# Down products in groups of four tiles, done between the Strassen pairs of the next group, and accumulators dealt out anew

## The chip, the core and the metric

The kernel runs on one core of a Trainium2 chip. The metric is the device time of one execution in microseconds; before the change the median of 3 runs is 2069.6 us (2067.61 to 2075.72).

## What is computed

A decoder trunk of two layers with model width 1024, on 512 tokens, float32. Each layer adds half a feed-forward, a mixer, and half a feed-forward again:

```python
x = x + 0.5 * swiglu_ffn(rmsnorm(x, g1), w_gu1, w_down1)
x = x + mixer(rmsnorm(x, gm))
x = x + 0.5 * swiglu_ffn(rmsnorm(x, g2), w_gu2, w_down2)
def swiglu_ffn(x, w_gu, w_down):
    gate, up = jnp.split(x @ w_gu, 2, axis=-1)
    return (jax.nn.silu(gate) * up) @ w_down
```

The hidden width is 2816, which is 22 tiles of 128. The change touches the feed-forward alone; it runs four times (stages f0a, f0b, f1a, f1b). The two mixers, the norms and the inputs are as they were.

## The kernel before, in words

The residual lies in X, eight tiles of 128 channels by 512 tokens. Every float32 product is made of three matmuls (`mm3`, L177 to L179): operands are split into a high part, written by ACT, and a low part, the DVE difference; weight-high times x-high, weight-high times x-low, weight-low times x-high.

A feed-forward (`ffn`) makes 22 hidden tiles. The first four (CLASSIC) are plain: gate and up are 24 matmuls of 512 columns each, and `hidden` makes the tile. The other 18 are *pairs* (class `Pair`): gate and up of one hidden tile are made together by seven Strassen-Winograd products (B11, Q7, Q6, B21, Q4, Q5, B22), each 12 matmuls of 256 columns, so 84 a pair. They multiply combinations of the four weight quarters, made on DVE in `load` (L311 to L313) from raw blocks that four DMAs bring (L307 to L310), with combinations of the activation quarters, made once per feed-forward by `Quarters.before` and `Quarters.after` (split at L260 to L264, combined at L269 to L282). `load` then makes four split weights ("jobs", L320 on ACT and L321 on DVE) in tiles given by `parts`, a ring of five. There are raw blocks for two pairs.

A pair has three accumulators: a and b from the ring `psum()` of PSB = 5, e from `psum2()` of 3. p1 makes a, and ACT copies it to b (L338). p7 makes e, copied to the upper half of t2 (L349). p6 goes on a, copied to the lower half of t2 (L354). p2 goes on b, and ACT takes its silu (L343). p4 goes on e, and DVE adds half of e to t2 (L359). p5 goes on a, ACT copies it to the free half of b (L364), and DVE adds that to t2 (L365). p3 goes on a; ACT takes the silu (L370), DVE multiplies (L372), and `down` writes the hidden tile's high part on ACT (L390) and its low part on DVE (L391).

Hidden tiles live in a ring of eight (NH). So the 22 tiles are done in groups of 8, 8 and 6: all pairs of a group, then the whole down product of the group: for each of the eight X tiles one accumulator over the group's tiles (24 or 18 matmuls of 512 columns), its weights by `wload` (L163, L171, L172), and one DVE addition into X (L458). Stages in the order of time are then: 4 pairs (after the 4 plain tiles), down of 8, 8 pairs, down of 8, 6 pairs, down of 6. The third product p3 of a pair comes after p1 and p7 of the next one (`left`); the last pair of a group ends p5, p4, p3.

The order on PE is the program's order (`manual_schedule(engines=PE_ONLY)`). On ACT, DVE and the queues a planner orders the instructions ahead of time by a modelled time and a priority; `high_priority(offset=n)` gives an instruction the priority of one n places earlier. Offsets: raw blocks and combinations RAHEAD = 400, splits SAHEAD = 230 (180 and 110 for the first two pairs), evictions EV = 320, the hidden tile's multiply and split 160, `wload` 90. Each engine then runs its list in that order, whatever the chip's real times.

Of the kernel before, what the change touches and what calls it, by code (L numbers as in the profile page):

```python
# [12 lines left out]
P = 128  # L13
T = 512
# [42 lines left out]
def build(tc, a, out, stages=("f0a", "ab", "f0b", "f1a", "nsa", "f1b")):  # L57
    nc = tc.nc
    with ExitStack() as ctx:
# [16 lines left out]
        def blk(i, dt, name):  # L76
            return bp.tile([P, BW.get(i, 4 * T)], dt, name=name, tag=f"b{i}")
# [8 lines left out]
        def psum():  # L86
            return pp.tile([P, T], F32, name="ps", bufs=PSB)
# [33 lines left out]
        def roots(after):  # L121

            nc.scalar.activation(warm, after[:, 0:1], AF.Sqrt, scale=0.0, bias=eps)
# [42 lines left out]
        def wload(src, n=CW, eng=None):  # L166
            with tc.high_priority(offset=AHEAD):
                raw = wraw(src, n)
                hi = wp.tile([P, CW], F32R, name="whi")
                lo = wp.tile([P, CW], F32R, name="wlo")  # L170
                nc.scalar.activation(hi[:, :n], raw[:, :n], AF.Copy)  # L171
                (eng or nc.vector).tensor_sub(lo[:, :n], raw[:, :n], hi[:, :n].bitcast(F32))  # L172
            return hi, lo

        def mm3(ps, wh, wl, xh, xl, start, stop, on=False):

            nc.tensor.matmul(ps, wh, xh, start=start, stop=False, skip_group_check=on)  # L177
            nc.tensor.matmul(ps, wh, xl, start=False, stop=False, skip_group_check=on)  # L178
            nc.tensor.matmul(ps, wl, xh, start=False, stop=stop, skip_group_check=on)  # L179
# [116 lines left out]
        class Pair:  # L296
# [1 line left out]
            def __init__(self, Q, down):  # L298
                self.Q, self.down, self.W = Q, down, {}

            def load(self, w, rb, first=False):
                with tc.high_priority(offset=RFIRST if first else RAHEAD):
                    ra, rc = (blk(rb[2 * (turns[1] % 2) + i], F32, f"r{i}")[:, :4 * T]
                              .rearrange("p (s c) -> p s c", s=4) for i in range(2))
                    turns[1] += 1

                    nc.sync.dma_start(ra[:, 0], w[0][:, :T])  # L307
                    nc.sync.dma_start(rc[:, 3], w[1][:, :T])
                    nc.sync.dma_start(ra[:, 3], w[1][:, T:])
                    nc.sync.dma_start(rc[:, 0], w[0][:, T:])  # L310
                    nc.vector.tensor_add(ra[:, 1:3], ra[:, 0:4:3], rc[:, 3:4].to_broadcast([P, 2, T]))  # L311
                    nc.vector.tensor_add(rc[:, 1], ra[:, 0], ra[:, 2])
                    nc.vector.tensor_add(rc[:, 2], rc[:, 0], rc[:, 1])  # L313
                with tc.high_priority(offset=SFIRST if first else SAHEAD):
                    for src, names in ((ra[:, 0:2], ("B11", "Q7")), (rc[:, 0:2], ("B21", "Q6")),
                                       (ra[:, 2:4], ("Q5", "Q4")), (rc[:, 2:3], ("B22",))):
                        hi, lo = parts()
                        m = len(names) * T
                        src = src.rearrange("p s c -> p (s c)")
                        nc.scalar.activation(hi[:, :m], src, AF.Copy)  # L320
                        nc.vector.tensor_sub(lo[:, :m], src, hi[:, :m].bitcast(F32))  # L321
                        for n, name in enumerate(names):
                            self.W[name] = hi[:, n * T:(n + 1) * T], lo[:, n * T:(n + 1) * T]
                return self
# [7 lines left out]

            def p1(self):

                self.a, self.b, self.t1 = psum(), psum(), tp.tile([P, T], F32, name="t1", bufs=3)
                self.product(self.a, "B11", True)
                with tc.high_priority(offset=EV):
                    nc.scalar.activation(self.b[:, :H], self.a[:, :H], AF.Copy)  # L338
# [16 lines left out]

            def p4(self):
                self.product(self.e, "Q4", False)
                with tc.high_priority(offset=EV):
                    nc.vector.tensor_add(self.t2[:, :H], self.e[:, :H], self.t2[:, :H])  # L359

            def p5(self):
                self.product(self.a, "Q5", False)
                with tc.high_priority(offset=EV):
                    nc.scalar.activation(self.b[:, H:], self.a[:, :H], AF.Copy)  # L364
                    nc.vector.tensor_add(self.t2[:, H:], self.b[:, H:], self.t2[:, H:])  # L365

            def p3(self):
                self.product(self.a, "B22", False)
# [6 lines left out]
        def ffn(gname, wgu, wd, x, lay, nxt, first=None):  # L375
# [30 lines left out]
            for j in range(CLASSIC):  # L406
# [19 lines left out]
                    quarters.before()  # L426
                if j >= 2:
                    hidden(*wait.pop(0))
            quarters.after()

            left = []
            j0 = 0
            while j0 < JT:
                j1 = min(JT, j0 + NH)
                js = list(range(max(CLASSIC, j0), j1))
                with tc.manual_schedule(engines=PE_ONLY):
                    if js[0] == CLASSIC:

                        p, q = (Pair(quarters.Q, downs(j)).load(wgu[j], rb, True) for j in js[:2])
                        for f in (p.p1, p.p7, p.p6, q.p1, q.p7, p.p2, p.p4, p.p5, q.p6, p.p3, q.p2, q.p4, q.p5):  # L440
                            f()
                        left = [q.p3]
                        js = js[2:]
                    for j in js:
                        p = Pair(quarters.Q, downs(j)).load(wgu[j], rb)
                        end = j == j1 - 1
                        for f in (p.p1, p.p7, *left, p.p6, p.p2, *((p.p5, p.p4, p.p3) if end else (p.p4, p.p5))):
                            f()
                        left = [] if end else [p.p3]
                if j1 == JT:  # L450
                    roots(hpart(JT - 1)[0].bitcast(F32))
                for i in range(KT):
                    ps = psum()
                    hi, lo = wload(wd[i, :, j0 * P:j1 * P], (j1 - j0) * P)
                    for k in range(j1 - j0):
                        mm3(ps, hi[:, k * P:(k + 1) * P], lo[:, k * P:(k + 1) * P], *hpart(k),
                            k == 0, k == j1 - j0 - 1)
                    nc.vector.scalar_tensor_tensor(X[i], ps, 0.5, X[i], op0=OP.mult, op1=OP.add)  # L458
                    if j1 == JT:
                        nxt(i)  # L460
                j0 = j1

        def out_proj(w, yh, yl, nxt, lead):

# [818 lines left out]
```

## Time and profile before

| | |
|---|---|
| median of 3 runs | 2069.6 us |
| the profiled execution | 2072.72 us, span 2071.0 us |
| PE / PEld busy | 1991.6 / 1735.3 us |
| DVE / ACT / POOL busy | 1373.8 / 1028.7 / 278.0 us |
| mean granted TensorE clock | 0.985 of full |
| four feed-forwards, from the first pair on | 59.6 to 381.1, 656.4 to 965.6, 1011.4 to 1318.9, 1746.8 to 2053.7 us |

Busy times are shares of one execution; a line such as L177 is that of a helper and is told apart by the operand (h: down product; qB, qQ: pairs; x: plain tiles and projections). Times of a timeline row are the start and the length; in square brackets stands the idle time of the engine before it, and what ended that.

### The profile page before, as it was taken

How to read it: one execution, taken by the hardware profiler on the slowest of the kernel's cores; microseconds unless marked ns; L12 is line 12 of the kernel's file. 1: busy time of each engine (PE TensorE's matmuls, PEld its weight loads, DVE VectorE, ACT ScalarE, POOL GpSimd, SP SyncE). 2: the span in 40 equal slices, each digit the busy share in tenths (PEclk: the TensorE clock that was granted, in tenths of full speed). 3: DMA queues.
4: the chain of work that ended last, by engine and by line, in shares of the span. 5: the costliest groups of instructions: out<-in, count | busy, mean ns of one | idle time of the engine just before them, and what ended most of it. 6: DMA issues, size and time to landing. Idle time of an engine off the chain costs nothing.

```text
span 2071.0 us, 30532 instructions
## 1 busy us (share of the span) xinstructions
PE 1991.6 (96%) x11896; PEld 1735.3 (84%) x11896; DVE 1373.8 (66%) x2189; ACT 1028.7 (50%) x1900; POOL 278.0 (13%) x290
## 2 busy tenths in 40 slices
PE   8899899989999998999999999999999999999997
PEld 6889898867788998897989889877777768999896
DVE  6847657489758658475956746433877778657474
ACT  5525436355545445254535435334878755445252
POOL 3000000343020000002000000202655530000002
PEclk9999999999999999999999999999999999999998
DMA  5232322322222333233232323321101032323222
GB/s 184 83 101 82 112 79 77 99 72 87 82 97 89 115 90 112 69 110 109 84 112 85 111 85 113 106 90 51 34 16 32 16 107 81 113 87 108 87 62 87
DMA packets 74736, 182.09 MB, mean 88 GB/s; under 512 B 8416, under 2 KB 9184, under 8 KB 74592
## 3 DMA queue, kind: packets, MB, share of 16 engines
q1 hardware_dynamic: 74448, 180.06, 28.0%
q8 instruction: 93, 1.52, 0.3%
q14 instruction: 51, 0.42, 0.1%
q10 hardware_dynamic: 144, 0.09, 0.0%
HBM read 178.02 MB, written 2.10 MB: 87 GB/s over the span
## 4 chain that ended last, share of the span: by engine, by line
PE 60%; DVE 9%; DMA 4%; issue 3%; ACT 2%; POOL 0%; SPq 0%; POOLq 0%; DVEq 0%; ACTq 0%
PE ps L177 14%; PE ps L178 14%; PE ps L179 14%; DMA r<-wgu 3%; PE pt L179 3%; PE pt L177 3%; PE pt L178 3%; PE px L994 2%; PE pt L789 2%; PE pt L1010 1%; DVE wx L321 1%; PE ps L954 1%; PE pt L1011 1%; DVE wlo L172 1%; DVE wlo L321 1%
## 5 line engine op out<-in xcount | busy, mean ns | idle before, releaser
L171 ACT ACTIVATE whi<-raw 128x1024 fp32r<-128x1024 f32 (+2 forms) x196 | 193.2, 987 | 363.9 <-PE ps L178 251.6
L178 PE MATMUL ps<-h,whi 128*128 128x512 f32 x704 | 277.5, 394 | 1.2 <-DVE h L391 1.2
L177 PE MATMUL ps<-h,whi 128*128 128x512 f32 x704 | 275.8, 392 | 1.0 <-ACT h L390 1.0
L179 PE MATMUL ps<-h,wlo 128*128 128x512 f32 x704 | 275.9, 392 | 0.0
L320 ACT ACTIVATE whi<-r 128x1024 fp32r<-128x1024 f32 (+1 forms) x174 | 165.6, 952 | 194.3 <-PE ps L178 156.5
L172 DVE TENSOR_TENSOR wlo<-raw,whi 128x1024 fp32r<-128x1024 f32 (+2 forms) x166 | 192.4, 1162 | 73.3 <-ACT whi L171 68.4
L118 POOL TENSOR_TENSOR acc<-acc,t 128x512 f32<-128x512 f32 x48 | 74.6, 1555 | 1136.4 <-ACT t L116 1131.2
L458 DVE SCALAR_TENSOR_TENSOR X<-ps,X 128x512 f32<-128x512 f32 x96 | 66.4, 691 | 231.0 <-PE ps L179 231.0
L321 DVE TENSOR_TENSOR wlo<-r,whi 128x1024 fp32r<-128x1024 f32 (+1 forms) x174 | 188.8, 1087 | 23.0 <-ACT whi L320 22.5
L177 PE MATMUL ps<-x,whi 128*128 128x512 f32 x432 | 179.0, 414 | 0.9 <-ACT x L106 0.9
L311 DVE TENSOR_TENSOR r<-r,r 128x1024 f32<-128x1024 f32 x72 | 88.9, 1236 | 134.2 <-DMA r<-wgu 134.0
L179 PE MATMUL ps<-x,wlo 128*128 128x512 f32 x432 | 171.1, 396 | 0.0
L178 PE MATMUL ps<-x,whi 128*128 128x512 f32 x432 | 170.7, 395 | 0.4 <-DVE x L107 0.3
L177 PEld LDWEIGHTS ps<-h,whi 128*128 128x128 f32 x704 | 132.9, 189 | 31.4 <-ACT h L390 1.9
L178 PEld LDWEIGHTS ps<-h,whi 128*128 128x128 f32 x704 | 132.9, 189 | 30.5 <-DVE h L391 2.4
L179 PEld LDWEIGHTS ps<-h,wlo 128*128 128x128 f32 x704 | 132.7, 188 | 28.5
L177 PE MATMUL ps<-qB,whi 128*128 128x256 f32 x520 | 145.8, 280 | 3.4 <-ACT ps L364 3.4
L179 PE MATMUL ps<-qB,wlo 128*128 128x256 f32 x520 | 145.1, 279 | 0.3 <-DVE wlo L321 0.3
L178 PE MATMUL ps<-qB,whi 128*128 128x256 f32 x520 | 145.2, 279 | 0.0
L321 DVE TENSOR_TENSOR wx<-r,wx 128x1024 fp32r<-128x1024 f32 (+1 forms) x114 | 123.4, 1083 | 22.4 <-ACT wx L320 19.2
L390 ACT ACTIVATE h<-t 128x512 fp32r<-128x512 f32 x88 | 55.4, 630 | 144.7 <-DVE t L372 142.1
L320 ACT ACTIVATE wx<-r 128x1024 fp32r<-128x1024 f32 (+1 forms) x114 | 107.2, 941 | 6.1 <-DVE r L311 4.1
(340 smaller groups left out, 5457.3 us busy)
## 6 DMA issues: line engine op xcount, KB each, us to landing
r<-wgu SPq DMA_DIRECT2D x288, 256.0 KB, 3.7
raw<-wd SPq DMA_DIRECT2D x64, 512.0 KB, 3.6
raw<-wgu SPq DMA_DIRECT2D x30, 512.0 KB, 3.5
raw<-wd SPq DMA_DIRECT2D x32, 384.0 KB, 3.1
raw<-ab_fm SPq DMA_DIRECT2D x21, 512.0 KB, 3.5
raw<-nsa_fm SPq DMA_DIRECT2D x17, 512.0 KB, 3.4
raw<-ab_out SPq DMA_DIRECT2D x8, 512.0 KB, 3.5
raw<-nsa_out SPq DMA_DIRECT2D x16, 256.0 KB, 2.7
```

The source lines that it names most:

```text
L118: nc.gpsimd.tensor_add(acc, acc, sq)
L171: nc.scalar.activation(hi[:, :n], raw[:, :n], AF.Copy)
L172: (eng or nc.vector).tensor_sub(lo[:, :n], raw[:, :n], hi[:, :n].bitcast(F32))
L177: nc.tensor.matmul(ps, wh, xh, start=start, stop=False, skip_group_check=on)
L178: nc.tensor.matmul(ps, wh, xl, start=False, stop=False, skip_group_check=on)
L179: nc.tensor.matmul(ps, wl, xh, start=False, stop=stop, skip_group_check=on)
L311: nc.vector.tensor_add(ra[:, 1:3], ra[:, 0:4:3], rc[:, 3:4].to_broadcast([P, 2, T]))
L320: nc.scalar.activation(hi[:, :m], src, AF.Copy)
L321: nc.vector.tensor_sub(lo[:, :m], src, hi[:, :m].bitcast(F32))
L390: nc.scalar.activation(hh, t2, AF.Copy)
L458: nc.vector.scalar_tensor_tensor(X[i], ps, 0.5, X[i], op0=OP.mult, op1=OP.add)
L789: nc.tensor.matmul(p2[m][:, :155].rearrange("p (g n) -> p g n", g=5), w[:, q * 256 + m * P:q * 256 + (m + 1) * P], tt[:, :, n:n + 8 * 30 + ...
```

## The change

`load` can be made in two parts, so that a down weight's tile can be taken between the first job and the other three. Accumulator b comes from the ring of three. The copy after p5 goes to the free half of e, and `second` makes one 512-wide addition of e to t2 when both p4 and p5 are done. `quarters.after` has a priority 120 places earlier. The function `two` loads the down weights of two X tiles for a group of four hidden tiles in one transfer, splits them, and gives two functions, each an accumulator of 12 matmuls and one addition into X. They are called between the products of the pairs: tiles 0 to 3 in the first four pairs, tiles 4 to 7 in pairs 8 to 11, and so on to tiles 12 to 15 in pairs 16 to 19; pairs 20 and 21 have none. The down product of tiles 16 to 21 follows at the end as before.

```diff
-            def load(self, w, rb, first=False):
...
+            def load(self, w, rb, first=False, part=0):
...
+                    self.jobs = [(ra[:, 0:2], ("B11", "Q7")), (rc[:, 0:2], ("B21", "Q6")),
+                                 (ra[:, 2:4], ("Q5", "Q4")), (rc[:, 2:3], ("B22",))]
...
+                    for src, names in (self.jobs, self.jobs[:1], self.jobs[1:])[part]:
...
-                self.a, self.b, self.t1 = psum(), psum(), tp.tile([P, T], F32, name="t1", bufs=3)
+                self.a, self.b, self.t1 = psum(), psum2(), tp.tile([P, T], F32, name="t1", bufs=3)
...
             def p4(self):
                 self.product(self.e, "Q4", False)
-                with tc.high_priority(offset=EV):
-                    nc.vector.tensor_add(self.t2[:, :H], self.e[:, :H], self.t2[:, :H])
+                self.second()
...
-                    nc.scalar.activation(self.b[:, H:], self.a[:, :H], AF.Copy)
-                    nc.vector.tensor_add(self.t2[:, H:], self.b[:, H:], self.t2[:, H:])
+                    nc.scalar.activation(self.e[:, H:], self.a[:, :H], AF.Copy)
+                self.second()
+
+            def second(self):
+
+                self.n = getattr(self, "n", 0) + 1
+                if self.n == 2:
+                    with tc.high_priority(offset=EV):
+                        nc.vector.tensor_add(self.t2, self.e, self.t2)
...
+            with tc.high_priority(offset=120):
+                quarters.after()
+
+            def two(i, j0, j1):
+
+                n = (j1 - j0) * P
+                with tc.high_priority(offset=SAHEAD):
+                    raw = wp.tile([P, CW], F32, name="raw", bufs=2)[:, :2 * n]
+                    nc.sync.dma_start(raw.rearrange("p (i c) -> p i c", i=2),
+                                      wd[i:i + 2, :, j0 * P:j1 * P].rearrange("i p c -> p i c"))
+                    hi, lo = parts()
+                    nc.scalar.activation(hi[:, :2 * n], raw, AF.Copy)
+                    nc.vector.tensor_sub(lo[:, :2 * n], raw, hi[:, :2 * n].bitcast(F32))
+
+                def one(m):
                     ps = psum()
...
+                        ks = slice(m * n + k * P, m * n + (k + 1) * P)
+                        mm3(ps, hi[:, ks], lo[:, ks], *hpart(j0 + k), k == 0, k == j1 - j0 - 1)
+                    nc.vector.scalar_tensor_tensor(X[i + m], ps, 0.5, X[i + m], op0=OP.mult, op1=OP.add)
+
+                return lambda: one(0), lambda: one(1)
+
+
+            G = 4
+            with tc.manual_schedule(engines=PE_ONLY):
+
+                p = Pair(quarters.Q, downs(CLASSIC)).load(wgu[CLASSIC], rb, True)
+                q = Pair(quarters.Q, downs(CLASSIC + 1))
+                q.load(wgu[CLASSIC + 1], rb, True, 1)
+                d = two(0, 0, G)
+                q.load(None, None, True, 2)
+                e = two(2, 0, G)
+                for f in (p.p1, p.p7, p.p6, q.p1, d[0], d[1], p.p2, q.p7, p.p4, p.p5, q.p6, p.p3, e[0], q.p2, e[1],
+                          q.p4, q.p5):
+                    f()
+                left = [q.p3]
+                for j in range(CLASSIC + 2, JT):
+                    p = Pair(quarters.Q, downs(j)).load(wgu[j], rb)
+                    j0 = min(j // G * G, JT - JT % G - G)
+                    i = 2 * (j - j0)
+                    d = two(i, j0 - G, j0) if i < KT else ((lambda: None),) * 2
+                    rest = (p.p5, p.p4, p.p3) if j == JT - 1 else (p.p4, p.p5)
+                    for f in (p.p1, p.p7, *left, d[0], p.p6, p.p2, d[1], *rest):
+                        f()
+                    left = [p.p3]
+            roots(hpart(JT - 1)[0].bitcast(F32))
```

Taken out is the loop over groups quoted in words above (pairs of a group, then its down product); the down product at the end keeps its form, with `hpart(j0 + k)`.

## Rows read from the trace of the kernel before

**Rows 1.** The page, part 1 (engines) and part 4 (chain that ended last).
```profile
PE 1991.6 (96%) x11896; PEld 1735.3 (84%) x11896; DVE 1373.8 (66%) x2189; ACT 1028.7 (50%) x1900; POOL 278.0 (13%) x290
...
PE 60%; DVE 9%; DMA 4%; issue 3%; ACT 2%; POOL 0%; SPq 0%; POOLq 0%; DVEq 0%; ACTq 0%
```

**Rows 2.** Waits of PE: who, for whom, us in total, times, longest.
```profile
PE ps L179 <- DVE wx L321: 10.8, 7, 2.1
...
PE ps L177 <- ACT ps L364: 10.0, 8, 2.7
...
PE ps L177 <- ACT t L354: 5.7, 3, 3.9
```

**Rows 3.** Windows of the four-pair stages: engine busy us (count), PEclk, DMA; sum.
```profile
59.60:108.70 49.10, 43.18 (x338) 42.44 (x338) 41.28 (x52) 27.42 (x47) 0.00 (x0) 0.93 0.35 100
...
656.40:695.90 39.50, 39.50 (x337) 39.29 (x336) 34.54 (x44) 27.42 (x46) 0.00 (x0) 1.00 0.30 94
...
sum 169.30, PE 162.14 PEld 160.58 DVE 147.75 ACT 107.65 POOL 0.00; mean PE 40.54 PEld 40.14 DVE 36.94 ACT 26.91 POOL 0.00
```

**Rows 4.** Windows of the four eight-pair stages, their sum and mean.
```profile
sum 343.60, PE 323.71 PEld 320.26 DVE 257.12 ACT 191.81 POOL 0.00; mean PE 80.93 PEld 80.06 DVE 64.28 ACT 47.95 POOL 0.00
```

**Rows 5.** Windows of the four six-pair stages, their sum and mean.
```profile
sum 243.10, PE 237.57 PEld 236.00 DVE 177.41 ACT 139.14 POOL 1.38; mean PE 59.39 PEld 59.00 DVE 44.35 ACT 34.78 POOL 0.34
```

**Rows 6.** Windows of the eight down stages of eight tiles; first, and sum.
```profile
108.70:152.60 43.90, 43.90 (x194) 36.03 (x193) 17.90 (x21) 9.41 (x11) 0.00 (x0) 1.00 0.35 105
...
sum 355.20, PE 354.09 PEld 289.89 DVE 144.76 ACT 73.79 POOL 0.00; mean PE 44.26 PEld 36.24 DVE 18.10 ACT 9.22 POOL 0.00
```

**Rows 7.** Windows of the four down stages of six tiles, their sum.
```profile
sum 133.90, PE 132.83 PEld 108.03 DVE 79.60 ACT 66.54 POOL 34.62; mean PE 33.21 PEld 27.01 DVE 19.90 ACT 16.64 POOL 8.65
```

**Rows 8.** Timeline of DVE in an eight-pair stage: start, us, instruction, idle.
```profile
232.84 1.23 DVE L311 TENSOR_TENSOR r<-r,r 128x1024 f32<-128x1024 f32 x1 [3.95 <-DMA r<-wgu]
...
233.98 0.69 DVE L372 TENSOR_TENSOR t<-t,t 128x512 f32<-128x512 f32 x1
...
236.32 0.68 DVE L391 TENSOR_TENSOR h<-t,h 128x512 fp32r<-128x512 f32 x1
```

**Rows 9.** Timeline of ACT, the same place.
```profile
229.03 0.39 ACT L370 ACTIVATE t<-ps 128x256 f32<-128x256 f32 x1
```

**Rows 10.** The page, part 5: two DVE groups, busy and mean ns, idle before.
```profile
L458 DVE SCALAR_TENSOR_TENSOR X<-ps,X 128x512 f32<-128x512 f32 x96 | 66.4, 691 | 231.0 <-PE ps L179 231.0
...
L311 DVE TENSOR_TENSOR r<-r,r 128x1024 f32<-128x1024 f32 x72 | 88.9, 1236 | 134.2 <-DMA r<-wgu 134.0
```

**Rows 11.** Waits of SP's own queue, the longest in total.
```profile
SPq L163 <- DVE wlo L172: 689.4, 153, 23.9
```

**Rows 12.** Groups by form: the 128x256 pieces of a pair's end.
```profile
L365 DVE TENSOR_TENSOR t<-ps,t 128x256 f32<-128x256 f32 x72 | 30.0, 417 | 4.3 <-ACT ps L364 4.3
...
L364 ACT ACTIVATE ps<-ps 128x256 f32<-128x256 f32 x72 | 26.5, 368 | 17.9 <-PE ps L179 17.9
```

**Rows 13.** Timeline of PE, first four-pair stage: wait for Q4.
```profile
72.35 0.38 PE L177 MATMUL pt<-qQ,whi 128*128 128x256 f32 x1 [3.90 <-ACT qQ L263]
```

**Rows 14.** Timeline of DVE there: low part of tile 3, Q4 subtract.
```profile
67.76 0.69 DVE L391 TENSOR_TENSOR h<-t,h 128x512 fp32r<-128x512 f32 x1
...
68.97 1.22 DVE L279 TENSOR_TENSOR xn<-xn,xn 128x1024 f32<-128x1024 f32 x1
```

**Rows 15.** Timeline of DVE, fourth feed-forward: the same tile's low part.
```profile
1754.16 0.69 DVE L391 TENSOR_TENSOR h<-t,h 128x512 fp32r<-128x512 f32 x1
```

**Rows 16.** Timeline of ACT at two group ends: silu of the last product.
```profile
109.71 0.36 ACT L370 ACTIVATE t<-ps 128x256 f32<-128x256 f32 x1
...
2020.95 0.39 ACT L370 ACTIVATE t<-ps 128x256 f32<-128x256 f32 x1 [0.69 <-PE ps L179]
```

**Rows 17.** Timeline of DVE at the same two: the hidden tile, low part.
```profile
112.71 0.69 DVE L391 TENSOR_TENSOR h<-t,h 128x512 fp32r<-128x512 f32 x1 [0.70 <-ACT h L390]
...
2023.29 0.68 DVE L391 TENSOR_TENSOR h<-t,h 128x512 fp32r<-128x512 f32 x1
```

More of the change, by code (lines that the diff above doesn't have):

```diff
@@ L299, in __init__ @@
                 self.Q, self.down, self.W = Q, down, {}
-            def load(self, w, rb, first=False):
[L302 to L313, printed above, removed]
+            def load(self, w, rb, first=False, part=0):
+                if part < 2:
+                    with tc.high_priority(offset=RFIRST if first else RAHEAD):
+                        ra, rc = (blk(rb[2 * (turns[1] % 2) + i], F32, f"r{i}")[:, :4 * T]
+                                  .rearrange("p (s c) -> p s c", s=4) for i in range(2))
+                        turns[1] += 1
+                        nc.sync.dma_start(ra[:, 0], w[0][:, :T])
+                        nc.sync.dma_start(rc[:, 3], w[1][:, :T])
+                        nc.sync.dma_start(ra[:, 3], w[1][:, T:])
+                        nc.sync.dma_start(rc[:, 0], w[0][:, T:])
+                        nc.vector.tensor_add(ra[:, 1:3], ra[:, 0:4:3], rc[:, 3:4].to_broadcast([P, 2, T]))
+                        nc.vector.tensor_add(rc[:, 1], ra[:, 0], ra[:, 2])
+                        nc.vector.tensor_add(rc[:, 2], rc[:, 0], rc[:, 1])
+                    self.jobs = [(ra[:, 0:2], ("B11", "Q7")), (rc[:, 0:2], ("B21", "Q6")),
+                                 (ra[:, 2:4], ("Q5", "Q4")), (rc[:, 2:3], ("B22",))]
                 with tc.high_priority(offset=SFIRST if first else SAHEAD):
-                    for src, names in ((ra[:, 0:2], ("B11", "Q7")), (rc[:, 0:2], ("B21", "Q6")),
-                                       (ra[:, 2:4], ("Q5", "Q4")), (rc[:, 2:3], ("B22",))):
+                    for src, names in (self.jobs, self.jobs[:1], self.jobs[1:])[part]:
                         hi, lo = parts()
@@ L428, in ffn @@
                     hidden(*wait.pop(0))
[L429 to L452, printed above, removed]
+            with tc.high_priority(offset=120):
+                quarters.after()
@@ L453, in ffn @@
                     ps = psum()
-                    hi, lo = wload(wd[i, :, j0 * P:j1 * P], (j1 - j0) * P)
                     for k in range(j1 - j0):
[L456 to L461, printed above, removed]
+                        ks = slice(m * n + k * P, m * n + (k + 1) * P)
@@ L463, in out_proj @@
+            roots(hpart(JT - 1)[0].bitcast(F32))
+            for i in range(KT):
+                ps = psum()
+                hi, lo = wload(wd[i, :, j0 * P:], (JT - j0) * P)
+                for k in range(JT - j0):
+                    mm3(ps, hi[:, k * P:(k + 1) * P], lo[:, k * P:(k + 1) * P], *hpart(j0 + k),
+                        k == 0, k == JT - j0 - 1)
+                nc.vector.scalar_tensor_tensor(X[i], ps, 0.5, X[i], op0=OP.mult, op1=OP.add)
+                nxt(i)
         def out_proj(w, yh, yl, nxt, lead):
```

## The prediction

> **What bounds the kernel now.** I read the page's engine line and chain first: PE is busy for 96% of the span, and 60% of the chain that ended last is PE, while DVE, DMA and "issue" have 9%, 4% and 3% [rows 1]. PE's work is not changed by this edit, so all that can be gained is time in which PE waits or runs at the lower clock inside the feed-forwards. The waits of PE name DVE's low parts of weights (10.8 us) and ACT copies and evictions (10.0 and 5.7 us) as the largest [rows 2]; all of these belong to pairs.
>
> Next I cut the four feed-forwards into stages and compared each kind of stage with its best member. The best four-pair stage takes 39.50 us, and there PE is busy throughout [rows 3]; that is 9.875 us a pair and 1.41 us a product. An eight-tile down stage takes 43.90 us for 192 matmuls [rows 6], which is 0.2286 us each, 2.74 us for twelve of them, and 32.9 us for the 144 of a six-tile stage. Against these floors: the four-pair stages 169.3 - 158.0 = 11.3 us [rows 3]; the eight-pair stages 343.6 - 316.0 = 27.6 us [rows 4]; the six-pair stages 243.1 - 237.0 = 6.1 us [rows 5]; the eight-tile down stages 355.2 - 351.2 = 4.0 us [rows 6]; the six-tile ones 133.9 - 131.7 = 2.2 us [rows 7]. Together 51.2 us, the most that better order in the feed-forwards can give. More than half lies in the eight-pair stages. Of the first stage's share, 9.6 us are f0a's alone (49.1 against 39.5): a wait of 3.90 us for the quarter Q4 [rows 13], and a mean granted clock of 0.93 where the best stage has 1.00 [rows 3], so that some 7 us ran at 1.2 instead of 2.4 GHz.
>
> Why a long run of pairs loses time can be seen on DVE. It isn't short of capacity: 257.1 us in 32 pairs, 8.0 us a pair, against 9.875 [rows 4]. But its list is in order, and at L311 it stands idle for the raw blocks, 134 us over 72 pairs [rows 10]. In one instance it waits 3.95 us, and the multiply of the pair before, whose silu was begun at 229.03, comes only behind that at 233.98 [rows 8, 9]. A block is reloaded only when its splits are done, these need a weight tile that PE gives back, and the two-pair buffer leaves no room when a pair lasts 9.9 us. So the pair stages run at the latency of that loop, not at the rate of an engine.
>
> **What the change does, part by part.**
>
> *Pairs stretched.* A pair with two down pieces takes 9.875 + 2 x 2.74 = 15.4 us. DVE's share becomes 8.0 + 1.24 (one more 128x1024 subtraction, priced as L311 [rows 10]) + 2 x 0.69 (two additions into X [rows 10]) - 0.16 (a 512-wide addition, near 0.69, for two of 0.417 [rows 12]) = 10.5 us, 68%. ACT has 191.8 / 32 = 6.0 us a pair [rows 4] and gets one more split, so under 8 of 15.4. Each pair and its down weight take five jobs, the length of the ring, so each job meets the tile freed a pair earlier, a lead of 7 to 14 us. A DMA wait of 4 us at L311 is then covered. I count the eight-pair loss as gone, 27.6 us, and two thirds of the six-pair loss, 4.1 us (pairs 20 and 21 have no down piece, and 2.0 us stay). The eight-tile down stages vanish as stages, and with them 4.0 us of start-up waits and low clock. The six-tile stage stays, with its 2.2.
>
> *More additions into X.* Forty instead of 24 per feed-forward: 64 x 0.69 = 44 us more on DVE in all [rows 10]. The cover is the 32% of DVE left in the slot, and five accumulators: two pairs hold a, two down pieces the others, one is spare. If that cover fails PE waits up to 0.69 us a piece. I take nothing.
>
> *Transfers.* The down weights are as many transfers as before, 16 of 512 KB and eight of 384 KB per feed-forward, but they are now issued between the raw blocks of the pairs on SP's one queue. SP already spends 689 us waiting for the raw tile to come free, up to 23.9 us at once [rows 11], and what is queued behind such a wait is the next pair's four blocks. They are wanted a pair and a half later, so I take nothing; the other end is in the third rival.
>
> *First two pairs.* The four pieces of 2.74 us stand ahead of p2 and of the last products, and `quarters.after` moves up. In f0a the Q4 subtract stood behind other work until 68.97 [rows 14]; PE now wants Q4 only after 59.6 + 7 x 1.41 + 5.5 = 75 us, which is late enough. New is that the first piece needs hidden tile 3: its low part is wanted four products and ten matmuls after the stage's start, 5.6 + 2.3 = 7.9 us. Before, it was finished after 8.85 us in f0a (67.76 + 0.69 - 59.6) and 8.05 us at the latest in the other three (1754.16 + 0.69 - 1746.8) [rows 14, 15], and the quarters now come in front of it. I keep 4.5 of f0a's 9.6 us (between 1.0, the tile as late as it was, and 9.6) and add 0.4 us to each other first stage, 1.2 us. Gone: 5.1.
>
> *Accumulator b in the ring of three.* Where two pairs are open at the start, p.b, p.e and q.b hold the ring, and q.p7 must wait for p.b, so for the silu right behind p2: 0.37 us of ACT [rows 12] and two hand-overs, about 0.6 us, four times, 2.4 us. The bounds are 0.37 and the longest wait of PE for such an ACT step, 2.7 us [rows 2]. In later pairs at most e of the last pair, b and e are alive: no wait.
>
> *The copy after p5 goes into e.* Normally nobody follows closely. In a feed-forward's last pair p4 is behind p5, and p4 writes the half of e beside the one that ACT is filling. If it has to wait: 0.5 us, four times, 2.0 us, from 0.37 for the copy [rows 12]; if not, nothing; at worst the ACT wait of 2.7 and p4's own 1.41 more, 16 us for four. I take 2.0. The Trainium skill, PSUM — Partial Sum Buffer, section "PSUM bank collisions raise a hardware error", says to guard by bank and quadrant, not by address: by that p4 waits and the 2.0 us stand, by address the sum is 2 us lower. No row here shows which.
>
> *Down right behind the group's last p3.* This is the large new cost. Pairs 8, 12 and 16 run p3 of the last pair of the group and then a piece over that group, of which the last tile is wanted after nine (high part) and ten matmuls (low part): 2.29 us after p3, about 2.24 after its silu starts. Before, 21 or 15 matmuls covered that. There are twelve group ends in the trace, as many as there will be such places. From the start of the silu (L370) to the end of the low part (L391) they took 3.69 us at the first (109.71 to 113.40) and 3.02 us at the last (2020.95 to 2023.97) [rows 16, 17]; the twelve run from 3.02 to 6.33, median 3.72. A stall of 1.48 us, twelve times: 17.8 us. The ends are 0.78 us each (the shortest), 9.4 us, and 5.7 us each: in the middle of a stage the same chain took 7.97 us (229.03 to 237.00), because of the L311 wait [rows 8, 9]. I take the median of the group ends, since they too have other casts in DVE's list but mostly no DMA wait.
>
> **Sum.** Gone: 27.6 + 4.1 + 4.0 + 5.1 = 40.8 us. New: 17.8 + 2.4 + 2.0 + 1.2 = 23.4 us. Net -17.4, from 2072.7 us of the profiled execution to 2055.3; that execution stands 3.1 us above the median, so **2052 us**, 0.85% less.
>
> **Rivals.**
>
> *Everything fits (2038 us).* The twelve stalls are the shortest, 9.4 us (-8.4), f0a keeps 1.7 instead of 4.5 (-2.8), p4 and tile 3 wait for nothing (-3.2). For it: DVE at 68% leaves the multiply and the low part less to stand behind. Against: in the planner's order they have a lower priority than splits and raw blocks.
>
> *Slower (2103 us).* DVE's list still has a wait at L311 in front of the multiply, at the three places in each feed-forward where PE now wants the tile at once. Then 12 x 5.73 = 68.8 us instead of 17.8: +51. For it: so it is in the middle of the stages now [rows 8, 9], where it cost little because nobody wanted the tile for many products. Against: B22's tile is freed by the very p3 from which the chain starts, so the block behind it can be reloaded only then, and L311 should come into the list after the chain. The point at which it decides: a mean stall of (17.8 + 17.4) / 12 = 2.9 us, so a low part 5.2 us after the silu, turns the gain into none.
>
> *The loop stays (2068 us).* The raw blocks come as late as before because SP's queue stands behind a down weight [rows 11], and half of the 31.7 us in pair stages stays: +15.9. Against it: a slot is half as long again as the loop now takes.
>
> **How the numbers follow.** Chances: the forecast 0.42 (its own range 2042 to 2064), everything fits 0.25, the loop stays 0.15, slower 0.18. A measurement of this kernel tells about 0.5%, 10.3 us, from no change: faster means under 2059, slower over 2080. Faster: four fifths of the forecast, all of the first rival, a little of the third, 0.61. Same: the rest of the forecast, most of the third and the mild end of the second, 0.23. Slower: 0.16. The range from 2032 to 2078 reaches a little below the first rival and past the third, and leaves out most of the second.
>
> **What would show it.** In the profile after: slots of 15.4 us between one p1 and the next with DVE near 68% and PE idle for little; PE's waits for weights' low parts nearly gone; L311's idle time no longer followed by a late PE; at pairs 8, 12 and 16 a PE wait for h (L390, L391) of about 1.5 us; one short wait per feed-forward at q.p7 for the silu of b; f0a's clock dip gone or halved. The prediction is wrong if the waits for h are over 2.9 us on the mean, or if pairs with down pieces last clearly over 15.4 us elsewhere.

## The result, and the profile after

| | before | after |
|---|---|---|
| median | 2069.43 us (4 runs) | 2160.07 us (4 runs, 2158.6 to 2166.16) |
| ratio of the runs | | 1.0436, interval 1.0411 to 1.0461 |
| profiled execution, span | 2071.0 us | 2158.6 us |
| mean granted TensorE clock | 0.985 | 0.971 |

The kernel became 4.4% slower, where 0.85% faster was forecast. The page's engine line answers to [rows 1]: as many PE instructions, 36 us more of PE's busy time, and a share that fell from 96% to 94%, so PE ran slower for part of the time and waited for more of it.

```profile
PE 2027.8 (94%) x11896; PEld 1750.8 (81%) x11896; DVE 1434.4 (66%) x2181; ACT 1040.5 (48%) x1900; POOL 278.3 (13%) x290
```

Next the four feed-forwards of the kernel after, from the first pair on: the window, its length, the busy time of PE, PEld, DVE, ACT and POOL, then the granted clock, DMA's share and GB/s.

```profile
60.20:372.80 312.60, 304.03 (x2041) 278.49 (x2040) 221.22 (x281) 153.06 (x246) 8.94 (x6) 0.99 0.32 95
646.80:1051.10 404.30, 337.76 (x2042) 299.03 (x2041) 217.24 (x256) 148.25 (x243) 8.98 (x6) 0.91 0.26 76
1096.80:1400.70 303.90, 299.20 (x2041) 274.29 (x2040) 213.20 (x249) 148.60 (x243) 10.56 (x12) 0.99 0.34 102
1831.70:2141.40 309.70, 303.74 (x2043) 277.69 (x2041) 212.06 (x247) 141.28 (x231) 8.27 (x6) 1.00 0.30 89
```

Before, the same four took 321.5, 309.2, 307.5 and 306.9 us. So f0a and f1a gained 8.9 and 3.6 us, f1b lost 2.8, and f0b alone lost 95.1: four calls of one function with the same instructions, of which one takes 100.4 us more than the third. PE sits idle there for 66.5 us (404.3 - 337.8) against 4.7, which is 61.8 us of the difference. The other 38.6 us is busy time: some 34 us of it go with a granted clock of 0.91 instead of 0.99 (against f0a, 337.8 - 304.0), and some 5 us with slower 256-column matmuls, by which f1a is ahead of f0a too (last section). What PE waits for stands in its waits (who, for whom, us in total, times, longest), which answer to [rows 2]:

```profile
PE ps L179 <- DVE wlo L450: 45.8, 15, 3.8
PE ps L177 <- ACT whi L449: 15.5, 15, 1.0
PE pt L177 <- DVE t L408: 6.2, 1, 6.2
PE ps L179 <- DVE wlo L324: 5.9, 2, 3.5
...
PE pt L177 <- ACT t L346: 4.4, 4, 1.3
PE ps L177 <- ACT h L399: 3.3, 4, 1.0
PE ps L178 <- DVE h L400: 2.9, 10, 0.9
```

L449 and L450 are ACT's high and DVE's low part of a down weight, in `two`. The waits for them, 61.3 us, all lie in f0b, and there are fifteen of each: one for every down weight that `two` loads (16 a feed-forward) but the first, which falls on a fixed place. Of the other lines, L313 is the first combination of a pair's raw blocks (L311 before), L323 and L324 are the two parts of a job (L320 and L321), L346 is p2's silu, L379 p3's, L381 the multiply, L399 and L400 are the two parts of the hidden tile, L408 is a plain tile's multiply. An experiment that adds or takes out lines moves such a number by one or two. The same view of f1a alone has no wait for a down weight:

```profile
PE ps L179 <- DVE wlo L324: 2.4, 1, 2.4
PE pt L177 <- ACT t L346: 1.3, 1, 1.3
PE ps L178 <- DVE h L400: 0.7, 3, 0.2
```

Windows of single slots (from one first down piece to the next) in f1a, f1b and twice in f0b, columns as above:

```profile
1258.50:1273.60 15.10, 15.10 (x111) 14.11 (x110) 11.23 (x14) 7.35 (x13) 0.00 (x0) 1.00 0.37 105
1947.80:1963.30 15.50, 15.50 (x110) 14.43 (x109) 11.21 (x13) 7.32 (x13) 0.00 (x0) 1.00 0.36 111
802.50:824.30 21.80, 17.55 (x109) 15.61 (x109) 11.12 (x13) 7.30 (x13) 0.00 (x0) 0.92 0.24 74
824.30:846.50 22.20, 18.32 (x108) 16.27 (x108) 11.12 (x13) 7.16 (x13) 0.00 (x0) 0.85 0.25 71
```

The forecast said 15.4 us for a slot, with DVE at 68%. Outside f0b that is what the slots do (15.1 to 15.5 us, DVE 72 to 74%, PE without a gap). In f0b a slot takes 6.3 to 7.1 us more, with the same work on DVE and ACT. The timelines of such a place (start, length, instruction, idle time before it and its releaser), ACT first, then DVE, then PE:

```profile
841.36 0.63 ACT L323 ACTIVATE whi<-r 128x512 fp32r<-128x512 f32 x1 [1.73 <-PE ps L178]
...
845.44 1.06 ACT L449 ACTIVATE whi<-raw 128x1024 fp32r<-128x1024 f32 x1
```

```profile
846.81 1.23 DVE L313 TENSOR_TENSOR r<-r,r 128x1024 f32<-128x1024 f32 x1 [3.49 <-DMA r<-wgu]
847.95 1.22 DVE L324 TENSOR_TENSOR wx<-r,wx 128x1024 fp32r<-128x1024 f32 x1
849.09 1.22 DVE L450 TENSOR_TENSOR wlo<-raw,whi 128x1024 fp32r<-128x1024 f32 x1
```

```profile
846.55 0.50 PE L177 MATMUL ps<-h,whi 128*128 128x512 f32 x1 [1.03 <-ACT whi L449]
850.36 0.50 PE L179 MATMUL ps<-h,wlo 128*128 128x512 f32 x1 [3.08 <-DVE wlo L450]
```

The down weight's high part is begun at 845.44, when the product before it on PE ends (846.55 - 1.03 = 845.52): its tile came free with the last product p3. Its low part then stands in DVE's list behind a combination L313 that waited 3.49 us for its blocks, and behind one more split. So of the 4.1 us that PE waits here (1.03 + 3.08), the late start of the high part has the first, and what DVE does in front of the low part has most of the second. In f1a the same two, from the timelines of ACT and of DVE, run 6.9 and 5.8 us ahead of the piece at 1273.6:

```profile
1266.70 1.06 ACT L449 ACTIVATE whi<-raw 128x1024 fp32r<-128x1024 f32 x1 [1.30 <-issue]
```

```profile
1267.80 1.23 DVE L450 TENSOR_TENSOR wlo<-raw,whi 128x1024 fp32r<-128x1024 f32 x1
```

**Where the four calls differ.** A feed-forward takes 18 x 4 jobs and 16 down weights from `parts`, 88 tiles, which is 3 more than a multiple of five. The count runs on through the program, so the feed-forwards begin at places 0, 3, 1 and 4 of the ring. Places 0, 1 and 2 are no fixed tiles: they are one tag with three buffers, and a buffer goes to whoever asks next in program order. Places 3 and 4 are fixed. The program's own addresses give the order in one slot (letters are tiles; the jobs are B11/Q7, B21/Q6, Q5/Q4, B22 and the down weight):

```
        B11/Q7  B21/Q6  Q5/Q4  B22  down
f1a  n    B       A       E     D    C       (E, D fixed)
     n+1  B       A       E     D    C
f0b  n    D       E       C     A    B       (D, E fixed)
     n+1  D       E       B     C    A
     n+2  D       E       A     B    C
```

In f1a each job meets its own tile of the pair before. In f0b the three buffers hold Q5/Q4, B22 and the down weight, and these change places: Q5/Q4 takes the tile that the down weight gave up, B22 takes that of Q5/Q4, and the down weight takes that of B22, which is read by p3, the product right before the down piece.

### The profile page after: what moved, and what is told of

Same layout as the page of the kernel before. It is cut to its first block, busy times and chain, and to the rows that moved or that the text cites. A ratio compares the mean times of both kernels' runs of the same rounds, so it can differ in the third digit from the quotient of the medians.

```text
span 2158.6 us, 30616 instructions
## 1 busy us (share of the span) xinstructions
PE 2027.8 (94%) x11896; PEld 1750.8 (81%) x11896; DVE 1434.4 (66%) x2181; ACT 1040.5 (48%) x1900; POOL 278.3 (13%) x290
## 4 chain that ended last, share of the span: by engine, by line
PE 62%; DVE 8%; DMA 3%; issue 3%; ACT 2%; POOL 0%; DVEq 0%; POOLq 0%; SPq 0%; ACTq 0%
PE ps L179 14%; PE ps L178 13%; PE ps L177 13%; PE pt L177 4%; PE pt L178 4%; PE pt L179 4%; DMA r<-wgu 3%; PE px L1025 2%; PE pt L820 2%; PE pt L1041 1%; DVE wlo L324 1%; PE ps L985 1%; DVE wlo L450 1%; PE pt L1042 1%; DVE wlo L172 1%
## 5 line engine op out<-in xcount | busy, mean ns | idle before, releaser
L323 ACT ACTIVATE whi<-r 128x1024 fp32r<-128x1024 f32 (+1 forms) x180 | 175.1, 973 | 205.8 <-PE ps L178 96.9
L324 DVE TENSOR_TENSOR wlo<-r,whi 128x1024 fp32r<-128x1024 f32 (+1 forms) x180 | 200.3, 1113 | 108.5 <-ACT whi L323 108.1
L179 PE MATMUL ps<-h,wlo 128*128 128x512 f32 x448 | 189.6, 423 | 45.8 <-DVE wlo L450 45.8
L171 ACT ACTIVATE whi<-raw 128x1024 fp32r<-128x1024 f32 (+2 forms) x132 | 125.4, 953 | 191.0 <-PE ps L178 100.2
L177 PE MATMUL ps<-h,whi 128*128 128x512 f32 x448 | 187.4, 418 | 15.9 <-ACT whi L449 15.5
L178 PE MATMUL ps<-h,whi 128*128 128x512 f32 x448 | 185.9, 415 | 0.7 <-DVE h L400 0.7
L324 DVE TENSOR_TENSOR wx<-r,wx 128x1024 fp32r<-128x1024 f32 (+1 forms) x108 | 113.8, 1054 | 81.3 <-ACT wx L323 79.9
L313 DVE TENSOR_TENSOR r<-r,r 128x1024 f32<-128x1024 f32 x72 | 88.9, 1236 | 111.8 <-DMA r<-wgu 108.8
L172 DVE TENSOR_TENSOR wlo<-raw,whi 128x1024 fp32r<-128x1024 f32 (+2 forms) x102 | 115.0, 1133 | 63.2 <-ACT whi L171 57.3
L179 PEld LDWEIGHTS ps<-h,wlo 128*128 128x128 f32 x448 | 91.1, 203 | 71.7 <-DVE wlo L450 52.3
L457 DVE SCALAR_TENSOR_TENSOR X<-ps,X 128x512 f32<-128x512 f32 x128 | 88.3, 690 | 61.8 <-PE ps L179 61.7
L177 PEld LDWEIGHTS ps<-h,whi 128*128 128x128 f32 x448 | 90.1, 201 | 37.8 <-ACT whi L449 18.5
L178 PE MATMUL ps<-qQ,whi 128*128 128x256 f32 x428 | 120.0, 280 | 0.0
L177 PE MATMUL ps<-qQ,whi 128*128 128x256 f32 x428 | 119.9, 280 | 0.0
L179 PE MATMUL ps<-qQ,wlo 128*128 128x256 f32 x428 | 119.8, 280 | 0.0
L399 ACT ACTIVATE h<-t 128x512 fp32r<-128x512 f32 x88 | 55.5, 631 | 124.0 <-DVE t L381 120.6
L323 ACT ACTIVATE wx<-r 128x1024 fp32r<-128x1024 f32 (+1 forms) x108 | 98.6, 914 | 25.6 <-issue 9.4
L177 PE MATMUL pt<-qQ,whi 128*128 128x256 f32 x360 | 101.5, 282 | 8.0 <-DVE t L408 6.2
```

What stands on the lines that cost most here:

```text
L457: nc.vector.scalar_tensor_tensor(X[i + m], ps, 0.5, X[i + m], op0=OP.mult, op1=OP.add)
```

## The experiments

Diffs are against the kernel after (in 8 and 9 against experiment 4). The first four ran on one chip (before: 2067.82 us), the next four on a second (2063.95), the last two on a third (2069.03). Experiment 1 was run ten times and experiment 6 four times; each of the others is a single run, and the kernel before spread from 2060 to 2073 us over 13 runs on the first chip. Small differences are therefore read from the feed-forwards' windows.

**1. Every feed-forward begins at place 1.**

```diff
             quarters = Quarters(gname, qb, hb[2:])
+            turns[0] += (1 - turns[0]) % 5
```

> Every feed-forward starts the ring of five split tiles at its second place, as f1a did by itself in the changed kernel (303.9 us there, against 404.3 in f0b, which started at the fourth). Theory A (place in the ring: in f0b the down weight shares the three-tile part of the ring with the jobs Q5/Q4 and B22, whose tiles come free in another order than they are asked for, so that the down weight can be split only when p3 has given up its tile, right before PE wants it): f0b falls by 95 to 100 us, the other three change by less than 8 each, and the whole takes 2050 to 2066 us. Rival B (f0b is slow because of its place in the program, its DMA waits at the block combinations or the in-order list of DVE): within 15 us of the changed kernel's 2160.

Measured: 2053.95 us (10 runs), ratio to before 0.9944, interval 0.9928 to 0.996. The windows of the four feed-forwards:

```profile
60.50:370.40 309.90, 299.04 (x2042) 274.58 (x2041) 221.54 (x281) 153.06 (x246) 8.96 (x6) 0.98 0.30 95
644.80:947.60 302.80, 297.66 (x2041) 272.50 (x2041) 218.93 (x257) 149.48 (x242) 8.92 (x6) 1.00 0.33 102
993.40:1296.90 303.50, 298.53 (x2042) 273.06 (x2041) 212.99 (x249) 148.61 (x243) 10.56 (x12) 1.00 0.33 103
1727.10:2035.50 308.40, 303.46 (x2042) 278.40 (x2041) 213.94 (x247) 141.57 (x231) 8.30 (x6) 1.00 0.28 88
```

f0b falls from 404.3 to 302.8 us, as theory A said, and the waits for L449 and L450 are gone. One line that moves only the start of a ring turns +4.4% into -0.6%.

**2. Every feed-forward begins at place 3.**

```diff
             quarters = Quarters(gname, qb, hb[2:])
+            turns[0] += (3 - turns[0]) % 5
```

> Every feed-forward starts the ring at its fourth place, as f0b did. Theory A: f0a, f1a and f1b each become as slow as f0b, 404 us instead of 304 to 313, and the whole takes 2160 + 90 + 100 + 95 = 2445 us (2400 to 2480). Rival B: within 15 us of 2160.

Measured: 2446.45 us, clock 0.924; feed-forwards of 409.3, 404.4, 403.4 and 399.9 us. Waits of PE:

```profile
PE ps L179 <- DVE wlo L451: 176.7, 60, 3.9
PE ps L177 <- ACT whi L450: 61.8, 60, 1.0
```

Four times fifteen slots now wait, 4.0 us each. Against experiment 1 the feed-forwards take 392.4 us more, 6.5 us a slot; the 2.5 us beyond the waits are busy time, most of it with the lower clock (0.90 and 0.91 in the four, against 0.98 to 1.00). The loss follows the start of the ring, not the place of f0b in the program.

**3. Own starts, the first down piece after p2.** The tile comes as late as ever, but its user two products later.

```diff
-                    for f in (p.p1, p.p7, *left, d[0], p.p6, p.p2, d[1], *rest):
+                    for f in (p.p1, p.p7, *left, p.p6, p.p2, d[0], d[1], *rest):
```

> The changed kernel with its own ring starts; the first down piece of a slot stands behind p6 and p2 instead of right behind p3, 2.8 us later. Theory A: the split that waits for p3 is the same, but 2.8 us of its 6.3 are covered in each of f0b's 15 slots (-42 us), and the waits at the group changes of the other three (0.9 to 1.9 us, nine of them) go (-11): about 2107 us (2095 to 2120). Rival B (DVE's list stands at the raw blocks, which come no earlier): less than 15 us gained.

Measured: 2088.66 us, 71.4 us less than after and 6 less than the theory's lower bound. f0b takes 341.9 us, and its waits:

```profile
PE ps L179 <- DVE wlo L450: 24.4, 15, 3.0
...
PE ps L177 <- ACT whi L449: 1.0, 1, 1.0
```

Two products are 2.7 us. PE's named waits in f0b fell by 35.9 us (61.3 to 25.4), less than 15 x 2.7; the granted clock there rose from 0.91 to 0.99 as well, which was not counted on: PE's busy time in f0b fell by 30 us (337.8 to 307.5), about half of the 62.4 us that f0b gained.

**4. Place 1, and `quarters.after` without its priority.**

```diff
+            turns[0] += (1 - turns[0]) % 5
...
-            with tc.high_priority(offset=120):
-                quarters.after()
+            quarters.after()
```

> As e1_start1, and the later activation quarters have their old priority. Theory: the 6.2 us wait of p7 in f0a for an accumulator, which the plain tile 3 still holds because its multiply stands behind the quarters on DVE, goes with its low clock (-7 to -9), and the waits for the first pairs' weights in f0b and f1a (3.5 and 2.4) fall: 4 to 14 us less than e1_start1. Rival: the quarter Q4 is late again in f0a, as before the change, and the time is within 3 us of e1_start1 or more.

Measured: 2035.45 us, 18.5 us less than experiment 1 and more than the theory's 4 to 14; feed-forwards of 300.3, 301.5, 300.3 and 305.2 us, 17.3 less in all. The waits for a plain tile's multiply (8.5 us there) and for L324 (6.7 us) are gone. The timelines of f0a's start show why; in the kernel after, with the priority, DVE and then PE:

```profile
62.05 1.21 DVE L261 SCALAR_TENSOR_TENSOR qB<-xn,qB 128x1024 fp32r<-128x1024 f32 x1
...
67.19 0.67 DVE L408 TENSOR_TENSOR t<-pt,R 128x512 f32<-128x512 f32 x1
```

```profile
67.91 0.58 PE L177 MATMUL pt<-qQ,whi 128*128 128x256 f32 x1 [6.18 <-DVE t L408]
```

Experiment 4, without it, DVE:

```profile
59.60 0.68 DVE L409 TENSOR_TENSOR t<-pt,R 128x512 f32<-128x512 f32 x1
...
66.78 1.22 DVE L261 SCALAR_TENSOR_TENSOR qB<-xn,qB 128x1024 fp32r<-128x1024 f32 x1
```

With the priority the quarters' combinations and splits (L261, L264, L279) go ahead of the plain tiles' last evictions, and the first pair's p7 waits for an accumulator that L408 gives back 7.7 us after the stage's start (67.86 - 60.2). Without it the last of these multiplies ends 1.6 us after that start (60.28 - 58.7), and they come behind.

**5. Experiment 4 with the late piece of experiment 3.** Does it take the waits at group changes away?

> As e4_start1_quarters (2035.5 us), and the first down piece of a slot stands behind p6 and p2. Theory: what is left of the price of going into a down piece right behind p3 is 0.9 us at each of the twelve group changes (high and low part of the last hidden tile late); 2.8 us more of other products cover it, so 11 us less: 2024 us (2020 to 2029). Rival: the piece then stands closer to the next one and the freed tiles come later, so that as much is lost at the splits: within 4 us of 2035.5.

Measured: 2027.11 us (298.6, 298.4, 298.7 and 302.3 us, 9.3 less than experiment 4 in all), within the theory's range. The wait for h (`DVE h L401`, 2.7 us in 12 in experiment 4) is gone.

**6. As 5, and in the first two pairs p2 between the two pieces, so that the silu of b is done when q.p7 wants its accumulator.**

```diff
-                for f in (p.p1, p.p7, p.p6, q.p1, d[0], d[1], p.p2, q.p7, p.p4, p.p5, q.p6, p.p3, e[0], q.p2, e[1],
+                for f in (p.p1, p.p7, p.p6, q.p1, d[0], p.p2, d[1], q.p7, p.p4, p.p5, q.p6, p.p3, e[0], q.p2, e[1],
```

> As e5_late, and in the first two pairs of a feed-forward the second down piece stands between p2 and q.p7, so that the silu of accumulator b, for which q.p7 waits (1.3 us four times in the changed kernel), lies beside it: 5 us less than e5_late, 2019 us (2014 to 2025). Rival: p2 then wants the quarter B21 2.7 us earlier and waits for that: no less than e5_late.

Measured: **2020.77 us** (4 runs, 2019.73 to 2021.88), ratio to before 0.9796, interval 0.976 to 0.9832: about 2% faster than the kernel before, and 6.7 us less in the four feed-forwards than experiment 5, near the 5 us expected. The windows of its four feed-forwards, their sum:

```profile
sum 1191.30, PE 1190.45 PEld 1099.80 DVE 863.62 ACT 584.30 POOL 36.71; mean PE 297.61 PEld 274.95 DVE 215.90 ACT 146.07 POOL 9.18
```

PE is busy for 1190.5 of 1191.3 us, at a granted clock of 1.00 in all four; almost nothing is left there for order to gain.

**7. Experiment 4 with b in the ring of five again, the copy after p5 into b and two half additions.**

> As e4_start1_quarters, with the accumulators dealt as before the change: b from the ring of five, the copy after p5 into b, two half-width additions. Theory: two pairs then hold four of the five and two down pieces of a slot want the fifth one after the other, so the second piece, or the next p1, waits for an addition into X of 0.7 us and its place in DVE's list, in each of the 16 slots with down pieces: 1 to 2 us each, 64 to 128 us more, 2100 to 2160. Rival: b is free soon enough behind p5, q.p7 no longer waits for a silu (5 us less), and the time is 2030 to 2036.

Measured: 2046.73 us, 11.3 us more than experiment 4 (15.2 more against each chip's own time before). Of this the four feed-forwards hold 9.0 us (306.6, 301.0, 303.0 and 305.7). Neither expectation holds as a whole, though the wait of q.p7 for the silu (5.1 us in experiment 4) is gone, as the rival said. The cost stands in one wait for each feed-forward, in its first two pairs, where a down piece finds no accumulator until the piece before it is added into X:

```profile
PE ps L177 <- DVE X L458: 10.7, 4, 4.4
```

In the later slots nothing waits for an accumulator. So dealing the accumulators out anew is worth those two pairs and no more.

**8, 9. Experiment 4 begun at place 0 and at place 2.**

```diff
-            turns[0] += (1 - turns[0]) % 5
+            turns[0] += (0 - turns[0]) % 5
```

> As e4_start1_quarters, but every feed-forward starts the ring at its first place, as f0a did in the changed kernel. The ring keeps its tiles in both. What is open is the step between products' matmuls, 114 ns where a feed-forward started at the second place and 117 to 118 at the others. If the place of the split weights sets it: f0a, f0b and f1a each get 84 x 16 x 3.5 ns = 4.7 us longer and more in the last pairs, 2050 us (2046 to 2054). If it was an accident of single runs: within 4 us of 2035.5.

Place 0: 2049.22 us, within the first range; 305.4, 304.8, 304.6 and 304.3 us. No wait of more than 1.4 us is new; what is longer is PE's busy time (last section).

> As e4_start1_quarters (2035.5 us), with the third place as the start of the ring in every feed-forward, which no kernel has run yet. The three-tile part then holds job B11/Q7, job B22 and the down weight; B22 is asked for before the down weight, takes the tile that the last down piece gave up, and the down weight must take B22's, which p3 gives up right before the next piece. Theory A: as slow as a start at the fourth place, 400 us a feed-forward, 2430 us in all (2400 to 2460). Rival (only f0b's start, or its three jobs together, are slow): 2035 to 2055.

Place 2 (in that line 2 for 0): 2140.62 us, which neither theory gave; 328.3, 327.6, 325.7 and 327.9 us. Waits of PE:

```profile
PE ps L177 <- ACT h L400: 27.2, 12, 2.7
PE ps L179 <- DVE wlo L450: 26.1, 57, 0.5
PE ps L178 <- DVE h L401: 9.2, 13, 0.8
```

Here too jobs change places, but the down weight gets a tile that p7 gives back, one product before p3, so it is late by 0.5 us and not 4. What is new is a wait for the hidden tile at each of the twelve group changes (three in each feed-forward, at pairs 8, 12 and 16, where the down pieces turn to the next four hidden tiles). DVE's timeline at one of them, where ACT had begun p3's silu at 129.59:

```profile
128.35 1.23 DVE L450 TENSOR_TENSOR wlo<-raw,whi 128x1024 fp32r<-128x1024 f32 x1 [1.26 <-ACT whi L449]
129.71 1.22 DVE L324 TENSOR_TENSOR wlo<-r,whi 128x1024 fp32r<-128x1024 f32 x1
131.42 1.22 DVE L313 TENSOR_TENSOR r<-r,r 128x1024 f32<-128x1024 f32 x1 [0.48 <-DMA r<-wgu]
132.56 0.68 DVE L381 TENSOR_TENSOR t<-t,t 128x512 f32<-128x512 f32 x1
```

The multiply comes 3 us after the silu began, behind two splits that were late and a combination that waited 0.48 us for its blocks. The same four stand in this order at all twelve; the combination waited 0.7 us at most, so the splits weigh more here. These waits, 62.5 us, are not the whole of the 102 us that the feed-forwards take more than in experiment 4; PE's busy time rose by 46 us, at a granted clock of 0.98 and with slower matmuls (last section).

**10. Experiment 4 begun at place 3, with the tag at places 3, 0 and 1 and the fixed tiles at 2 and 4.** Then the down weight (place 2) and B21/Q6 have tiles of their own, and B11/Q7, Q5/Q4 and B22 share the tag. The expectation below names Q5/Q4 and B22 as the jobs that still change places; by the program's addresses it is B11/Q7 and B22 that do, and Q5/Q4 keeps its tile.

```diff
-            if at < 3:
+            if at in (3, 0, 1):
...
-            t = blk(parts.blocks[at - 3], F32R, f"wx{at}")
+            t = blk(parts.blocks[at // 4], F32R, f"wx{at}")
...
+            turns[0] += (3 - turns[0]) % 5
```

> As e4_start1_quarters, with the slow fourth place as the start in every feed-forward, but the tiles dealt so that the down weight has a tile of its own and the jobs B11/Q7, Q5/Q4 and B22 share the three. In the built program Q5/Q4 and B22 then still change tiles from slot to slot. Theory A (what costs is that the down weight is split late, not the start and not that tiles change places): fast, 2035 to 2055 us. Rival (a start at the fourth place, or changing tiles, is slow by itself): 2400 or more.

Measured: 2108.53 us, again between the two; 316.7, 321.7, 318.3 and 320.6 us. Waits of PE:

```profile
PE ps L178 <- DVE h L401: 20.3, 12, 2.4
PE ps L177 <- ACT h L400: 17.5, 12, 1.5
...
PE ps L179 <- DVE wlo L450: 0.8, 2, 0.6
```

The waits for the down weight are gone (0.8 us in two), so they did come from its share in the exchange of tiles. The jobs that still swap make themselves felt at the twelve group changes, again in DVE's list: B11/Q7 takes the tile that p3 gives up, so its split (the first line) is ready only when the multiply and the low part want DVE. The silu was begun at 128.06:

```profile
128.19 1.23 DVE L324 TENSOR_TENSOR wlo<-r,whi 128x1024 fp32r<-128x1024 f32 x1 [1.09 <-ACT whi L323]
129.33 0.69 DVE L381 TENSOR_TENSOR t<-t,t 128x512 f32<-128x512 f32 x1
131.13 1.23 DVE L313 TENSOR_TENSOR r<-r,r 128x1024 f32<-128x1024 f32 x1 [1.11 <-DMA r<-wgu]
132.27 0.68 DVE L401 TENSOR_TENSOR h<-t,h 128x512 fp32r<-128x512 f32 x1
```

## Why the prediction was wrong

**The step that failed** is the one that let the stretched pair hide everything: "Each pair and its down weight take five jobs, the length of the ring, so each job meets the tile freed a pair earlier, a lead of 7 to 14 us." The count, five jobs for five places, is right, and the conclusion does not follow from it. Three of the five places are one tag, whose buffers are given out in the order of asking; and the ring's start differs from call to call, since 88 tiles are no multiple of five. Where every job gets its own tile back (f0a, f1a, f1b), the sentence holds. At place 3 the down weight's tile comes from p3 and its lead is nothing, and "A DMA wait of 4 us at L311 is then covered" fails with it: the low part is so late that it stands behind that wait. The forecast's own sign of being wrong, pairs with down pieces clearly over 15.4 us, is met in f0b's slots (21.8 and 22.2). Experiments 1 and 2 show that the start of the ring alone switches some 100 us for each feed-forward on and off, experiment 10 that the down weight's part in the exchange is the cause of most of it: with a tile of its own a feed-forward begun at place 3 takes 317 to 322 us and not 400 to 409. The code for this was all there before: `parts` and the count of jobs.

**The rest of the sum.** Experiment 1 is the change without this fault: 2053.95 us, where 2052 was forecast. By its terms:

- *Pairs stretched:* right. Slots of 15.1 to 15.5 us against 15.4, PE without gaps, although DVE has 11.2 us a slot and not 10.5. PE is idle for 4.7 us in the whole of f1a, so the losses of [rows 4, 5] are gone there, and L313's wait for blocks no longer makes PE late in such a slot.
- *Transfers:* right; no wait of PE ends with a down weight's transfer.
- *First two pairs:* wrong. Q4 is no longer what PE waits for [rows 13], but in its place stand the 6.18 us for L408, and 5.9 us in two other first stages for a weight's low part (L324). In experiment 1 f0a still takes 6 to 7 us more than f0b and f1a (309.9 against 302.8 and 303.5), where 4.5 us were to stay. What `quarters.after` is moved past was not priced: the multiplies that give the plain tiles' accumulators back. Taking the priority away is worth 18.5 us over the four (experiment 4). The fear was for tile 3's low part, for which PE hardly waited.
- *Silu of b before q.p7:* found as named, four times, mis-sized: 4.4 us against 2.4 (5.1 in experiments 4 and 5), and 6.7 us came back in experiment 6.
- *The copy after p5 into e:* found as named, in three feed-forwards of four. In f0b the matmul and its weight load waited at once, 1.3 and 1.7 us; in f1a and f1b the weight load alone, which runs beside matmuls, 0.3 us each. So 1.3 to 2.3 us, against 2.0. The view of L366 by source, who waited for it (us, times):

```profile
  PEld pt L177: 2.2, 3
  PE pt L177: 1.3, 1
```

That fits the rule that the forecast took from the Trainium skill, PSUM — Partial Sum Buffer, "PSUM bank collisions raise a hardware error". The wait is one that the program asks for; no run here shows whether the chip would have needed it.
- *Down right behind the group's last p3:* right in kind, too dear. In f1a the first piece after a group change takes 3.65 us instead of 2.75, in f1b 4.6 instead of 2.8; so 0.9 and 1.8 us against 1.48. In experiment 1 it is 0.9 each, 11 us instead of 17.8.
- *Together:* that experiment 1 comes out 2 us from the forecast is in part luck. Three of its feed-forwards run their pairs at 114 ns a matmul and not 118 (last section). By PE's busy time in experiments 4 and 8 (297.6 to 298.6 us against 302.1 to 302.2) that is some 4 us each, which no term held and which pay for two thirds of the priority. Experiment 8, which has neither, comes to 2049.22 us.

**The rivals.** "Everything fits" with 2038 us is what experiment 4 reaches (2035.45), after two edits that the change did not make. "Slower" with 2103 us got the sign of the result, but not its place: in the kernel after, PE waits only 6.2 us for h in fourteen waits. Its mechanism is real all the same: begun at place 2, or at 3 with the down weight apart, L313 does stand in front of the multiply or the low part at all twelve group changes (36.4 and 37.8 us of waiting), which the forecast had argued away by B22's tile being freed late. But the late splits beside it have a good part of that: L313's own wait for its blocks was 0.7 us at most in the one run and 0.2 to 1.7 us in the other. "The loop stays" did not happen for the reason given, SP's queue behind a down weight. In f0b L313 does wait for blocks, but these were asked for late: the transfer was issued at 840.91, right behind the split that ended at 840.88.

## What to carry to other kernels

That a pool has as many buffers as an iteration has requests says nothing yet: write down for one iteration who asks for a buffer, whose buffer that is and which instruction gives it back, and do it for every start that the counter can have at the loop's entry. When one function is called several times, compare its calls in the profile first; a loss in one of several identical calls points at state that is carried between them. And an edit that raises one step's priority is priced by what it is moved past, above all by evictions that give accumulators back.

## What was not expected of the hardware

The clock: with about 4 us of waiting in every slot of 22 us the granted clock of such slots was 0.85 and 0.92, so a part of them ran at 1.2 instead of 2.4 GHz: before the wait shown above 512-column matmuls started 0.23 us apart, behind it 0.43. With the 61.8 us of more idle time in f0b went some 34 us of more busy time. In experiment 3 the clock of f0b was 0.99 with 25.4 us of such waits.

The step from one 256-column matmul to the next differs between calls of one function, at the same granted clock. At 1.00 a slot without a wait takes 15.1 us in f1a and 15.5 in f1b, with the same instructions; in the kernel after, the median from one such matmul's start to the next is 114 ns in f1a and 118 in the three others. Begun at place 0 (experiment 8), f0a, f0b and f1a take 118 and some 305 us each; begun at place 1 (experiment 4), 114 and 300.3 to 301.5 us. In these three only tiles of weights differ between the two experiments. But f1b takes 118 or 119 with either. Nor is it a matmul's own tiles: in f0a many matmuls of B11, Q7, Q6 and B21 have the same weight, activation and accumulator tiles in both experiments, and still step by 114 in the one and 118 in the other. So the start of the ring goes with the difference in three calls, and the cause stays open.
